# A row softmax on one core: sixteen 4 MB tiles issued by a tile framework become eleven tiles of up to 6 MB, hand-synchronised and looped

## The chip, the core and the metric

The kernel runs on one core of a Trainium2 chip. The other cores are idle. The metric is the device time of one launch in microseconds (us); lower is better. The core has a matrix engine (PE, unused here except for waits in the changed kernel), a vector engine (DVE), an activation engine (ACT), a general engine (POOL) and a sequencer for transfers (SP). Sixteen DMA engines move data between the device memory (DRAM) and the on-chip memory (SBUF, 128 partitions).

## The reference: what is computed

```python
def setup_inputs():
    batch, seq, dim = 32, 512, 1024
    return {"x": np.random.randn(batch, seq, dim).astype(np.float32), "temperature": 0.5}

def reference(x, temperature):
    scaled = x / temperature
    shifted = scaled - np.max(scaled, axis=-1, keepdims=True)
    exp_x = np.exp(shifted)
    return (exp_x / np.sum(exp_x, axis=-1, keepdims=True)).astype(np.float32)
```

There are 16,384 rows of 1,024 float32 numbers, that is 67.1 MB to read and 67.1 MB to write. A row needs its maximum, the exponential of every element, the sum, and a multiplication by the reciprocal of the sum.

## The kernel before

The rows are cut into 16 tiles of 1,024 rows (`TILES = [[8]] * 16`, L10). A tile lies in SBUF as 128 partitions by 8 rows, and the 8 rows of a partition are neighbours in DRAM, so a partition's share is one run of 32 KB. Six buffers of 4 MB each (`BUFS = 6`, L11) hold the tiles, which are worked on in place. Each tile is computed in two groups of four rows a partition (`GROUP = 4`, L13).

For a group, `maximum` (L64) lets DVE take the four row maxima in one TENSOR_REDUCE (L70) and scale them into the exponential's bias (L73). `exponential` (L75) lets ACT run four ACTIVATE instructions (L79), one a row, each of which also leaves the row's sum. `divide` (L88) lets DVE take the four reciprocals (L91) and then multiply row by row (L93). `store` (L97) lets POOL issue one transfer of the whole tile to DRAM (L101) after the tile's second group, and then calls `load` for the tile that takes the same buffer.

The order on each engine is the order in which the Python loops emit the instructions (L107 to L116): the maximum and exponential of group g, then the divide and store of group g-1. All of it is unrolled, so DVE and ACT each have a stream of more than 200 instructions. The framework adds the semaphores. Loads are issued by SP (L61): six at the start, and each later one when the store that last read its buffer has landed. Stores go out through POOL's queue, loads through SP's queue.

After the last store, SP waits for the semaphores of everything that is in flight, POOL drains its queue, and all engines meet in a barrier, clear the semaphores and meet once more. The profile gives these instructions to L147.

Of the kernel before, what the change touches and what calls it, by code (L numbers as in the profile page):

```python
# [1 line left out]

# [4 lines left out]

TILES = [[8]] * 16  # L10
BUFS = 6  # L11

GROUP = 4  # L13


@with_exitstack
def kernel(
    ctx: ExitStack,
    tc: tile.TileContext,
    x: bass.AP,  # L20
    temperature: bass.AP,
    out: bass.AP,
):
    nc = tc.nc
    f32 = mybir.dt.float32
    scale = 1.0 / float(temperature)
    extreme = mybir.AluOpType.max if scale > 0 else mybir.AluOpType.min

    P = 128
    xf = x.flatten_outer_dims()  # L30
    of = out.flatten_outer_dims()
    n, d = xf.shape
    assert sum(sum(ks) for ks in TILES) * P == n

    data = ctx.enter_context(tc.tile_pool(name="data", bufs=BUFS))
    stats = ctx.enter_context(tc.tile_pool(name="stats", bufs=4))


    groups, first, r = [], [], 0
    for i, ks in enumerate(TILES):  # L40
        first.append(r)
        r += sum(ks)
        a = 0
        for k in ks:
            for b in range(0, k, GROUP):
                m = min(GROUP, k - b)
                groups.append((i, a + b, m, (a, k) if b + m == k else None))
            a += k

    def dram(t, i):  # L50
        k = sum(TILES[i])
        block = t[P * first[i] : P * (first[i] + k), :]
        return block.rearrange("(p k) d -> p k d", p=P, k=k)

    tiles, small = [], []

    def load():
        i = len(tiles)
        if i < len(TILES):
            xt = data.tile([P, sum(TILES[i]), d], f32, name="xt")  # L60
            nc.sync.dma_start(out=xt, in_=dram(xf, i))  # L61
            tiles.append(xt)

    def maximum(g):  # L64
        i, a, k, _ = groups[g]
        top, bias, sums, recip = (
            stats.tile([P, k], f32, name=name) for name in ("top", "bias", "sums", "recip")
        )
        small.append((bias, sums, recip))
        nc.vector.tensor_reduce(  # L70
            out=top, in_=tiles[i][:, a : a + k, :], axis=mybir.AxisListType.X, op=extreme
        )
        nc.vector.tensor_scalar_mul(bias, in0=top, scalar1=-scale)  # L73

    def exponential(g):  # L75
        i, a, k, _ = groups[g]
        bias, sums, _ = small[g]
        for b in range(k):
            nc.scalar.activation(  # L79
                tiles[i][:, a + b, :],  # L80
                tiles[i][:, a + b, :],
                mybir.ActivationFunctionType.Exp,
                bias=bias[:, b : b + 1],
                scale=scale,
                accum_out=sums[:, b : b + 1],
            )

    def divide(g):  # L88
        i, a, k, _ = groups[g]
        _, sums, recip = small[g]  # L90
        nc.vector.reciprocal(recip, sums)  # L91
        for b in range(k):
            nc.vector.tensor_scalar_mul(  # L93
                tiles[i][:, a + b, :], in0=tiles[i][:, a + b, :], scalar1=recip[:, b : b + 1]
            )

    def store(g):  # L97
        i, _, _, part = groups[g]
        if part:
            a, k = part  # L100
            nc.gpsimd.dma_start(out=dram(of, i)[:, a : a + k, :], in_=tiles[i][:, a : a + k, :])  # L101
            if a + k == sum(TILES[i]):
                load()

    with tc.manual_schedule():  # L107
        for _ in range(BUFS):
            load()
        for g in range(len(groups) + 1):  # L110
            if g < len(groups):
                maximum(g)
                exponential(g)
            if g > 0:
                divide(g - 1)
                store(g - 1)  # L116


# [1 line left out]
_INS = ['x', 'temperature']  # L120
_OUTS = [((32, 512, 1024), 'float32')]

_NUMBERS = {'temperature': 0.5}


# [26 lines left out]
```

## Time and profile before

| | |
|---|---|
| median of 10 runs | 318.36 us (318.01 to 318.74) |
| profiled execution, its own time | 318.1 us |
| profiled execution, span of the program's instructions | 316.3 us |
| DVE busy | 235.5 us (74%) |
| ACT busy | 149.6 us (47%) |
| POOL busy | 8.8 us (3%) |
| moved by DMA in the span | 134.25 MB, mean 424 GB/s |
| loads and stores | 16 and 16, of 4,096 KB each |

The profile is of one execution. Its times count from the first instruction of the program, and the span ends with the program's last instruction; some 1.8 us of the execution's own time lie outside the span. An engine's busy share tells how much of the span it works, not whether it decides the end. For a kernel that mostly moves data, the busy share of the DMA engines in slices of the span, and what happens before they start and after they stop, are the first things to read. Besides the loads (queue q1) and the stores (queue q0) there is a queue of instruction packets (q14), through which the engines' programs are fetched.

### The profile page before, as it was taken

To read this page: it belongs to the slowest core of one execution; us is meant where nothing else is said; L and a number is where in the kernel's file an instruction comes from. 1 tells how busy PE (TensorE), PEld (TensorE's weight loads), DVE (VectorE), ACT (ScalarE), POOL (GpSimd) and SP (SyncE) were. 2 spreads that over 40 slices of the span, in tenths; PEclk is the share of its full clock that TensorE was granted. 3 is DMA by queue.
4 is the path that set the end of the run, shared out by engine and by line. 5 is a ranking of instruction groups with operands and counts; after the bars stand their busy time and mean duration, and the time that the engine had idled before them with its cause. 6 is when DMAs were issued, how large, how long until landed. Compare 5 with 4: busy or idle time off the path is not lost.

```text
span 316.3 us, 639 instructions
## 1 busy us (share of the span) xinstructions
DVE 235.5 (74%) x224; ACT 149.6 (47%) x257; POOL 8.8 (3%) x20
## 2 busy tenths in 40 slices
DVE  0399999999698594976949679395893958949700
ACT  0176666666546065560645516355262553625500
POOL 0000000000000000000000000000000000000000
DMA  8999999999999999999999999999999999999995
GB/s 331 410 452 423 377 460 439 423 433 431 439 423 452 410 456 406 460 402 460 410 452 431 435 427 432 452 410 456 406 460 399 464 402 460 419 443 431 431 431 240
DMA packets 4612, 134.25 MB, mean 424 GB/s; under 512 B 512, under 2 KB 512, under 8 KB 512
## 3 DMA queue, kind: packets, MB, share of 16 engines
q1 hardware_dynamic: 2304, 67.11, 49.6%
q0 software_dynamic: 2304, 67.11, 49.2%
q14 instruction: 4, 0.03, 0.0%
HBM read 67.11 MB, written 67.11 MB: 424 GB/s over the span
## 4 chain that ended last, share of the span: by engine, by line
issue 88%; DMA 4%; POOL 2%; POOLq 0%
DMA xt<-in_x_dram 4%; POOL out_dram L101 2%; POOLq L147 0%; POOLq L101 0%
## 5 line engine op out<-in xcount | busy, mean ns | idle before, releaser
L79 ACT ACTIVATE xt<-xt,bias 128x1024 f32<-128x1024 f32 x128 | 145.4, 1137 | 135.3 <-DVE recip L91 117.9
L70 DVE TENSOR_REDUCE top<-xt 128x4 f32<-128x4096 f32 x32 | 141.3, 4416 | 61.0 <-DMA xt<-in_x_dram 61.0
L93 DVE TENSOR_SCALAR xt<-xt,recip 128x1024 f32<-128x1024 f32 x128 | 87.7, 750 | 1.1
L79 ACT ACTIVATION_READ_ACCUMULATOR xt<-xt,bias 128x1 f32 x128 | 23.8, 186 | 0.0
L101 POOL DMA_DIRECT2D out_dram<-xt x16 | 8.6, 540 | 292.6 <-DVE xt L93 292.6
L79 ACT ACT_TABLE_LOAD x1 | 1.3, 1283 | 13.0 <-DMA xt<-in_x_dram 13.0
L91 DVE RECIPROCAL recip<-sums 128x4 f32<-128x4 f32 x32 | 5.5, 171 | 2.1 <-ACT xt L79 2.1
L73 DVE TENSOR_SCALAR bias<-top 128x4 f32<-128x4 f32 x32 | 5.4, 170 | 1.1
L133 POOL MEMSET const-float32-0.0<- 128x1 f32 x1 | 0.1, 99 | 0.2 <-issue 0.2
L133 POOL MEMSET const-bfloat16-1.0<- 128x1 bf16 x1 | 0.1, 102 | 0.0
L133 POOL MEMSET const-float32-1.0<- 128x1 f32 x1 | 0.1, 99 | 0.0
L133 POOL MEMSET const-uint8-127<- 128x1 uint8 x1 | 0.1, 99 | 0.0
## 6 DMA issues: line engine op xcount, KB each, us to landing
xt<-in_x_dram SPq DMA_DIRECT2D x16, 4096.0 KB, 48.5
out_dram<-xt POOLq DMA_DIRECT2D x16, 4096.0 KB, 39.5
```

The costliest lines, as they stand in the source:

```text
L70: nc.vector.tensor_reduce(out=top, in_=tiles[i][:, a : a + k, :], axis=mybir.AxisListType.X, op=extreme)
L73: nc.vector.tensor_scalar_mul(bias, in0=top, scalar1=-scale)
L79: nc.scalar.activation(tiles[i][:, a + b, :], tiles[i][:, a + b, :], mybir.ActivationFunctionType.Exp, bias=bias[:, b : b + 1], scale=scal ...
L91: nc.vector.reciprocal(recip, sums)
L93: nc.vector.tensor_scalar_mul(tiles[i][:, a + b, :], in0=tiles[i][:, a + b, :], scalar1=recip[:, b : b + 1])
L101: nc.gpsimd.dma_start(out=dram(of, i)[:, a : a + k, :], in_=tiles[i][:, a : a + k, :])
L133: nc = _bacc.Bacc("TRN2", target_bir_lowering=False, num_devices=1)
```

## The change

The tiles become ten of 12 rows a partition and a last one of 8. They live in one buffer of four slots of 12 rows ("ring"). The framework's scheduling is replaced by one hand-written section with semaphores of its own.

SP issues the loads one after another; from the fifth on, each waits for the store that last read its slot. The first load is split into two transfers: partitions 0 to 15, and partitions 16 to 127 (`AHEAD = 16`). PE executes no arithmetic; it waits for each load's semaphore in turn and then adds 1 to a counter `ready`. POOL waits for the third load before it issues the first store, and then issues the first ten stores, each when all groups of its tile are scaled. SP issues the eleventh store.

DVE runs a loop over the tiles. Inside it, one loop over the tile's groups does maxima and biases, and a second does reciprocals and multiplications, so a tile's maxima all come ahead of its divisions. ACT runs a loop over tiles and, inside, over groups. The addresses are computed in registers. Counters that a loop waits for are counted down again by the wait (`take`). A small exponential is issued on ACT ahead of its loop. At the end, the hand-written section is left without a drain of POOL, and a second section waits for the eleventh store.

```diff
-TILES = [[8]] * 16
-BUFS = 6
+TILES = [12] * 10 + [8]
+SLOTS = 4
 GROUP = 4
+AHEAD = 16
...
+    pool = ctx.enter_context(tc.tile_pool(name="data", bufs=1))
+    ring = pool.tile([P, SLOTS * most, d], f32, name="ring")
...
+    def slot(i):
+        first = most * (i % SLOTS)
+        return ring[:, first : first + TILES[i], :]
+    def take(engine, sem, count=1):
+        engine.wait_ge(sem, count).then_inc(sem, -count)
+    def loop_groups(engine, t):
+        if groups[-1] == groups[0]:
+            return engine.Fori(0, groups[0])
+        short = t // (tiles - 1) * (groups[0] - groups[-1])
+        return engine.Fori(0, groups[0] - short)
-    with tc.manual_schedule():
-        for _ in range(BUFS):
-            load()
-        for g in range(len(groups) + 1):
-            if g < len(groups):
-                maximum(g)
-                exponential(g)
-            if g > 0:
-                divide(g - 1)
-                store(g - 1)
+    with tc.tile_critical(no_gpsimd_drain=True):
+        for i in range(tiles):
+            if i >= SLOTS:
+                nc.sync.wait_ge(stored[i % SLOTS], 16 * (i // SLOTS))
+            if i == 0:
+                nc.sync.dma_start(
+                    out=slot(0)[:AHEAD], in_=dram(xf, 0)[:AHEAD]
+                ).then_inc(opened, 16)
+                nc.sync.dma_start(
+                    out=slot(0)[AHEAD:], in_=dram(xf, 0)[AHEAD:]
+                ).then_inc(loaded[0], 16)
+            else:
+                nc.sync.dma_start(out=slot(i), in_=dram(xf, i)).then_inc(loaded[i % SLOTS], 16)
+        nc.tensor.wait_ge(opened, 16)
+        for i in range(tiles):
+            nc.tensor.wait_ge(loaded[i % SLOTS], 16 * (i // SLOTS + 1)).then_inc(ready, 1)
+        nc.gpsimd.wait_ge(loaded[2], 16)
+        for i in range(tiles - 1):
+            nc.gpsimd.wait_ge(scaled, sum(groups[: i + 1]))
+            nc.gpsimd.dma_start(out=dram(of, i), in_=slot(i)).then_inc(stored[i % SLOTS], 16)
+        with nc.vector.Fori(0, tiles) as t:
+            first = t % SLOTS * most
+            take(nc.vector, ready)
+            with loop_groups(nc.vector, t) as g:
+                group = bass.ds(g * GROUP, GROUP)
+                nc.vector.tensor_reduce(
+                    out=top[:, group],
+                    in_=ring[:, bass.ds(first + g * GROUP, GROUP), :],
+                    axis=mybir.AxisListType.X,
+                    op=extreme,
+                ).then_inc(topped, 1)
+                take(nc.vector, topped)
+                nc.vector.tensor_scalar_mul(
+                    bias[:, group], in0=top[:, group], scalar1=-scale
+                ).then_inc(biased, 1)
+            with loop_groups(nc.vector, t) as g:
+                group = bass.ds(g * GROUP, GROUP)
+                take(nc.vector, summed)
+                nc.vector.reciprocal(recip[:, group], sums[:, group]).then_inc(inverted, 1)
+                take(nc.vector, inverted)
+                for b in range(GROUP):
+                    row = ring[:, bass.ds(first + g * GROUP + b, 1), :]
+                    ins = nc.vector.tensor_scalar_mul(
+                        row, in0=row, scalar1=recip[:, bass.ds(g * GROUP + b, 1)]
+                    )
+                ins.then_inc(scaled, 1)
+        nc.scalar.activation(
+            warm, nc.const_aps.tensor(0.0, (P, 1)), mybir.ActivationFunctionType.Exp
+        )
+        with nc.scalar.Fori(0, tiles) as t:
+            first = t % SLOTS * most
+            with loop_groups(nc.scalar, t) as g:
+                take(nc.scalar, biased)
+                for b in range(GROUP):
+                    row = ring[:, bass.ds(first + g * GROUP + b, 1), :]
+                    column = bass.ds(g * GROUP + b, 1)
+                    ins = nc.scalar.activation(
+                        row,
+                        row,
+                        mybir.ActivationFunctionType.Exp,
+                        bias=bias[:, column],
+                        scale=scale,
+                        accum_out=sums[:, column],
+                    )
+                ins.then_inc(summed, 1)
+        i = tiles - 1
+        nc.sync.wait_ge(scaled, sum(groups))
+        nc.sync.dma_start(out=dram(of, i), in_=slot(i)).then_inc(finished, 16)
+        for i in range(tiles - SLOTS, tiles - 1):
+            nc.sync.wait_ge(stored[i % SLOTS], 16 * (i // SLOTS + 1))
+    with tc.tile_critical(no_gpsimd_drain=True):
+        nc.sync.wait_ge(finished, 16, synchronizes=[nc.sync.lower_ap(slot(tiles - 1))])
```

More of the change, by code (lines that the diff above doesn't have):

```diff
@@ L32 @@
     n, d = xf.shape
[L33 to L48, printed above, removed]
@@ L50, in dram @@
-    def dram(t, i):
[L51 to L67, printed above, removed]
-        )
[L69 to L102, printed above, removed]
-                load()
-    with tc.manual_schedule():
-        for _ in range(BUFS):
-            load()
-        for g in range(len(groups) + 1):
-            if g < len(groups):
-                maximum(g)
-                exponential(g)
-            if g > 0:
-                divide(g - 1)
-                store(g - 1)
+    tiles, most = len(TILES), max(TILES)
@@ new lines @@
+    assert sum(TILES) * P == n and all(k % GROUP == 0 for k in TILES)
+    groups = [k // GROUP for k in TILES]
+    assert all(g == groups[0] for g in groups[:-1]) and groups[-1] <= groups[0]
+    pool = ctx.enter_context(tc.tile_pool(name="data", bufs=1))
+    ring = pool.tile([P, SLOTS * most, d], f32, name="ring")
+    top = pool.tile([P, most], f32, name="top")
+    bias = pool.tile([P, most], f32, name="bias")
+    sums = pool.tile([P, most], f32, name="sums")
+    recip = pool.tile([P, most], f32, name="recip")
@@ new lines @@
+    warm = pool.tile([P, 1], f32, name="warm")
+    loaded = [tc.alloc_semaphore(f"loaded{s}") for s in range(SLOTS)]
+    stored = [tc.alloc_semaphore(f"stored{s}") for s in range(SLOTS)]
+    opened, ready, topped, biased, summed, inverted, scaled, finished = (
+        tc.alloc_semaphore(name)
+        for name in (
+            "opened", "ready", "topped", "biased", "summed", "inverted", "scaled", "finished",
+        )
+    )
+    def dram(t, i):
+        rows = t[P * sum(TILES[:i]) : P * sum(TILES[: i + 1]), :]
+        return rows.rearrange("(p k) d -> p k d", p=P, k=TILES[i])
@@ new lines, in slot @@
+    def slot(i):
[56 more added lines that the diff above has]
+            warm, nc.const_aps.tensor(0.0, (P, 1)), mybir.ActivationFunctionType.Exp
+        )
+        with nc.scalar.Fori(0, tiles) as t:
[12 more added lines that the diff above has]
+                        accum_out=sums[:, column],
+                    )
+                ins.then_inc(summed, 1)
[4 more added lines that the diff above has]
+            nc.sync.wait_ge(stored[i % SLOTS], 16 * (i // SLOTS + 1))
```

## The prediction, made before the changed kernel ran

> **What bounds the kernel now.** I read first the page's slices and queues, because the kernel computes little for each byte. The digits are the busy tenths of the DMA engines; a queue's line gives packets, MB and its share of sixteen engines' span.
>
> ```profile
> DMA  8999999999999999999999999999999999999995
> ...
> q1 hardware_dynamic: 2304, 67.11, 49.6%
> q0 software_dynamic: 2304, 67.11, 49.2%
> q14 instruction: 4, 0.03, 0.0%
> ```
>
> Loads (q1) and stores (q0) together take 98.8% of all sixteen engines' time; only the first and the last slice are not full. Next the table of stretches (us; then busy time of DVE, ACT and POOL; the clock; the DMA share; GB/s).
>
> ```profile
> 0.00:1.00 1.00, 0.00 (x0) 0.00 (x0) 0.20 (x4) 1.00 0.00 0
> 1.00:13.00 12.00, 0.01 (x1) 0.00 (x0) 0.00 (x0) 1.00 0.97 393
> ...
> 40.00:290.00 250.00, 200.10 (x191) 126.61 (x219) 7.44 (x14) 1.00 1.00 432
> ...
> 304.00:313.00 9.00, 0.00 (x0) 0.00 (x0) 0.00 (x0) 1.00 0.95 411
> 313.00:316.30 3.30, 0.00 (x0) 0.00 (x0) 0.00 (x0) 1.00 0.03 10
> ```
>
> The middle runs at 432 GB/s with no gap, so 134.2 MB cost 310.7 us whatever the engines do. Only some 5.6 us of the span are something else: about 2 at the start and 3 at the end. Then the waits:
>
> ```profile
> DVE top L70 <- DMA xt<-in_x_dram: 61.0, 12, 13.0
> ```
>
> ```profile
> SPq L61 <- DMA out_dram<-xt: 225.2, 10, 53.6
> ```
>
> DVE waits for loads, and loads wait for a buffer's store; no engine holds the transfers up. Last, what stands at the end: the timeline's last store, and the closing line's own instructions (ns, first and last start).
>
> ```profile
> 298.09 2.74 DVE L93 TENSOR_SCALAR xt<-xt,recip 128x1024 f32<-128x1024 f32 x4
> 301.13 0.53 POOL L101 DMA_DIRECT2D out_dram<-xt  x1 [11.72 <-DVE xt L93]
> ```
>
> ```profile
> L147 SPq EVENT_SEMAPHORE  x11: 17/28/28, 314.9 to 316.3; - x11
> L147 POOLq EVENT_SEMAPHORE  x4: 17/17/17, 315.6 to 316.2; - x4
> L147 POOLq DRAIN  x3: 34/101/14465, 301.1 to 316.1; - x3
> ```
>
> The last store is issued at 301.1 and is 9.7 us of transfer at 432 GB/s, yet transfers run to past 313: it found some 2.4 us of older stores ahead of it, so no gap opened.
>
> I also followed the trace's packet records engine by engine. A packet is one partition's 32,768 B and takes 1,213 ns; a completion packet of 4 B takes 9 ns. Fourteen engines write their last byte's completion at 313.0 to 313.4, the other two at 314.16 and 314.51. Those two carried the four instruction packets of q14 (8,192 B, 309 ns each, at 65.0, 65.0, 192.5 and 240.0), two each, and the data packet after each was 0.2 to 0.4 us late. So the kernel's last 1.1 us are two of sixteen engines finishing alone. Every engine's first packet took about 1.95 us, and around the first store (35 to 37) every engine lost about another 0.7 us.
>
> [...]
>
> **Part by part.** The sum is made against the profiled execution: 318.1 us, of which 316.3 are the span; the median of the runs is 0.26 above it.
>
> *Loops in short programs.* No engine's program reaches far enough to fetch while data flows, so the two late engines end with the others: 314.5 - 313.4 = 1.1 us less, all on the path.
>
> *Larger packets.* A partition's run becomes 48 KB. An engine's packets fall from 256 to 2 x (10 x 8 + 8) = 176. If each has a fixed part, it is at most the 9 ns of a 4-byte packet: 80 x 9 = 0.7 us; at least nothing. I take 0.4 us less.
>
> *DVE and ACT.* A group costs DVE 288.49 - 281.10 = 7.39 us by the timeline. The loop adds, for a group, two waits of DVE on itself, two loop ends[...], and register arithmetic. In the trace a dependent hop between engines is 30 to 40 ns and SP's waits follow each other every 61 ns; I estimate 0.25 to 0.3 for each self-wait with its lost overlap[...], 0.85 in all, bounds 0.3 and 1.8. The cover: a tile's load and store are 12.58 MB, 29.1 us, against 3 x 8.25 = 24.8 us of DVE. It is used up when first landing + 32 groups + last store fill the transfers' span: the first tile lands at 0.74 + 2.5 (the 12.2 of the first landing before less 9.7) + 14.6 = 17.8, so (313.5 - 17.8 - 11.2) / 32 = 8.9 us a group, 1.5 above today. Below that the cost is nothing; beyond it each 0.1 us costs 3.2. ACT has 4.6 us a group and stays shorter. The exponential put ahead and PE's counting (a hop of 0.04 us) lie beside the first transfer and cost nothing; without cover the table load is 1.3 us.
>
> *The first store's extra wait.* On POOL all later stores are queued behind it, and SP's fifth load waits for its landing. The third tile lands at 17.8 + 2 x 14.6 = 47; the four slots hold loads until 60, so transfers never run dry: nothing. Its second tile is ready by about 70 and the first store lands near 76, so the store queue is fed too. Without this cover each us of delay would cost one. The 0.7 us lost around the first store I leave as they are.
>
> *Last store on SP.* It is moved out of POOL's queue, behind loads that are all issued by then. The last load (4.2 MB) lands near 270, DVE is free at 276, and two groups bring the store to 292 or 293, with some 11 us of the tenth store still to move beside it: more cover than the 2.4 us of before.
>
> *Ends.* Before, SP walked through nine more waits (9 x 61 ns = 0.55 us) after the last landing, POOL's drain ended at 315.57, and two barriers followed, 0.25 and 0.45 us. Removed: about 0.5 us. Added: the leave of one section and the entry and leave of a second, 0.25 to 0.45 each, partly while the last store still moves. Bounds 0.6 better and 1.0 worse; I take 0.2 better. At the start, entering the section may cost a barrier (0.3 us), while a first transfer of 16 packets should be issued sooner than one of 128 (372 ns of issue before; up to 0.3): bounds 0.4 either way, I take 0.1 better.
>
> Sum: 1.1 + 0.4 + 0.2 + 0.1 = 1.8 us less, 316.3 for the profiled execution and 316.5 for the median.
>
> **Rivals.** *Few ports for the first 16 partitions (slower).* The place is the first load. [...] It decides as soon as that first packet costs over 1.8 us extra. [...] Against: no run here shows that engines sharing a port stall each other at this size.
>
> *The ends eat the gain.* If the three section edges cost 0.4 each on the path, the start 0.3 more and larger packets bring nothing: 318.4 - 1.1 + 1.2 - 0.5 + 0.3 = 318.3. For it: each barrier in the trace is of that size. Against: most edges can pass while stores move.
>
> *DVE becomes the bound.* At 1.8 us added a group: 316.5 + 3 x 3.2 = 326. For it: DVE is the busiest engine, 74%. Against: most register work can run while 0.75 us multiplications do.
>
> *The loops fetch after all.* Some 80 back-edges at about 0.6 us on one engine (309 ns and the late packet): up to 48 us, 340 and more. Against: bodies are short.
>
> **How the numbers follow.** Forecast 0.55; ports 0.20; ends 0.11; DVE 0.10; fetches 0.04. The likeliest case's own range is 315.5 to 317.7 (all bounds good: 1.1 + 0.7 + 0.6 + 0.4 less). The range reaches to 323.5 to take in most of the ports' case; what it leaves out is most of DVE's and the fetches' and the edges of the others. A measurement of this kernel can tell about 0.2%, 0.64 us, from no change: faster 0.55, same 0.12, slower 0.33.
>
> **What would show it.** In the changed profile: q14 without packets after the first microseconds, all engines' last completions within 0.5 us; 48 KB packets near 1.82 us; DVE groups near 8.25 us and DVE still waiting for loads; the last store issued near 292; SP's first issue near 0.7 to 1.0. The ports' case shows as a low DMA rate in the first 10 us[...]. The forecast is wrong if the middle drops below 432 GB/s, or a gap opens between stores at the end.

## The result, and the profile after

The changed kernel takes 333.23 us (333.04 to 333.83), the kernel before 318.32 in the runs beside it: a ratio of 1.047, interval 1.0461 to 1.0479. That is slower by 14.9 us and outside the predicted range of 315.5 to 323.5. The profiled execution took 333.48 us, of which 331.7 are the span.

The page after, slices and queues:

```profile
DMA  9989999999999999999999999999999999999996
...
q1 hardware_dynamic: 1744, 71.30, 54.8%
q0 software_dynamic: 1440, 62.92, 43.8%
```

The DMA engines look as busy as before: loads and stores together have 98.6% of their time, against 98.8%, and the queue of instruction packets is gone. A busy DMA engine is not a moving one, though. The table of stretches (us; then busy time of DVE, ACT and POOL; the clock; the DMA share; GB/s) shows it:

```profile
1.00:13.00 12.00, 0.00 (x0) 1.40 (x2) 0.00 (x0) 1.00 1.01 160
13.00:33.00 20.00, 0.00 (x0) 0.00 (x0) 0.00 (x0) 1.00 0.99 253
33.00:40.00 7.00, 4.52 (x2) 0.00 (x0) 0.00 (x0) 1.00 0.93 400
40.00:290.00 250.00, 211.18 (x198) 136.74 (x236) 4.92 (x9) 1.00 1.00 432
...
318.00:330.00 12.00, 0.00 (x0) 0.00 (x0) 0.00 (x0) 1.00 0.87 354
```

From 40 us on the rate is that of before, 432 GB/s. In the first 33 us it is 160 and then 253, at a DMA share of 0.99 to 1.01. Before, the first of these stretches ran at 393 GB/s, and the second was this:

```profile
13.00:33.00 20.00, 19.65 (x17) 13.61 (x22) 0.04 (x1) 1.00 1.02 441
```

The waits of DVE and POOL follow from that. L70 is the line of the helper `take`, so "DVEq L70" stands for a wait of DVE on one of the kernel's own counters; ahead of the first row maximum of a tile (`top`, L109) that is the wait for the tile's load.

```profile
POOL out_dram L102 <- DMA ring<-in_x_dram: 63.5, 1, 63.5
DVE top L109 <- DVEq L70: 35.2, 1, 35.2
```

DVE's first row maximum starts at 35.2 us instead of 13.0. It waits once, for the first tile, and never for a load again: 61.0 us of waits for loads before, 35.2 now, all at the start. Its work then goes on without a long gap to the last store, here from the timeline:

```profile
35.23 4.42 DVE L109 TENSOR_REDUCE top<-ring  x1 [35.23 <-DVEq L70]
39.90 0.17 DVE L116 TENSOR_SCALAR bias<-top  x1 [0.24 <-DVEq L70]
...
40.82 4.42 DVE L109 TENSOR_REDUCE top<-ring  x1 [0.75 <-issue]
...
316.70 0.35 SPq L155 DMA_DIRECT2D out_dram<-ring  x1
```

That is (316.70 - 35.23) / 32 = 8.80 us a group of four rows, of which there are 32. Two stories fit so far: the transfers were 15 us behind from the start and never won them back, or DVE, started late and slowed by its loop, set the end.

### The profile page after: what moved, and what is told of

The parts are those of the page before. It is cut to its first block, busy times and chain, and to the rows that moved or that the text cites. A ratio compares the mean times of both kernels' runs of the same rounds, so it can differ in the third digit from the quotient of the medians.

```text
span 331.7 us, 1879 instructions
## 1 busy us (share of the span) xinstructions
DVE 237.5 (72%) x224; ACT 149.9 (45%) x258; POOL 5.7 (2%) x14
## 5 line engine op out<-in xcount | busy, mean ns | idle before, releaser
L142 ACT ACTIVATE ring<-ring,bias x128 | 145.4, 1136 | 162.3 <-ACTq L70 162.3
L109 DVE TENSOR_REDUCE top<-ring x32 | 141.4, 4418 | 50.5 <-DVEq L70 35.2
L126 DVE TENSOR_SCALAR ring<-ring,recip x128 | 87.7, 749 | 13.2 <-DVEq L70 13.2
L142 ACT ACTIVATION_READ_ACCUMULATOR ring<-ring,bias x128 | 23.9, 187 | 0.0
L122 DVE RECIPROCAL recip<-sums x32 | 5.5, 173 | 8.0 <-DVEq L70 8.0
L116 DVE TENSOR_SCALAR bias<-top x32 | 5.5, 171 | 7.4 <-DVEq L70 7.4
L102 POOL DMA_DIRECT2D out_dram<-ring x10 | 5.5, 545 | 292.7 <-DVE ring L126 229.2
```

Source lines behind the costliest of these rows:

```text
L102: nc.gpsimd.dma_start(out=dram(of, i), in_=slot(i)).then_inc(stored[i % SLOTS], 16)
L109: nc.vector.tensor_reduce(out=top[:, group], in_=ring[:, bass.ds(first + g * GROUP, GROUP), :], axis=mybir.AxisListType.X, op=extreme,).th ...
L116: nc.vector.tensor_scalar_mul(bias[:, group], in0=top[:, group], scalar1=-scale).then_inc(biased, 1)
L122: nc.vector.reciprocal(recip[:, group], sums[:, group]).then_inc(inverted, 1)
L126: ins = nc.vector.tensor_scalar_mul(row, in0=row, scalar1=recip[:, bass.ds(g * GROUP + b, 1)])
L142: ins = nc.scalar.activation(row, row, mybir.ActivationFunctionType.Exp, bias=bias[:, column], scale=scale, accum_out=sums[:, column],)
```

## The experiments

The ratios are to the kernel before, run on the same chip beside each. "Ports" in the expectations is the author's name for a supposition: that a transfer's rate depends on which partitions it spans. No run here shows any ports.

### The first load as one transfer

```diff
-                nc.sync.dma_start(
-                    out=slot(0)[:AHEAD], in_=dram(xf, 0)[:AHEAD]
-                ).then_inc(opened, 16)
-                nc.sync.dma_start(
-                    out=slot(0)[AHEAD:], in_=dram(xf, 0)[AHEAD:]
-                ).then_inc(loaded[0], 16)
+                nc.sync.dma_start(out=slot(0), in_=dram(xf, 0)).then_inc(loaded[0], 16)
...
-        nc.tensor.wait_ge(opened, 16)
```

> The changed kernel with its first load as one transfer over 128 partitions. Theory 1 (ports: the split of the first load costs some 15 us of all transfers, the trace shows 160 GB/s in the first 12 us and 253 in the next 20): 316.5 to 318, first tile landed near 18 us, rate 432 GB/s from the start. Theory 2 (the looped engines or the section's edges cost the time, the slow first load being hidden by four slots of buffers): 330 or more.

Measured: 319.42 us, ratio 1.0036 (1.0024 to 1.0048). Its stretches:

```profile
1.00:13.00 12.00, 0.00 (x0) 1.40 (x2) 0.00 (x0) 1.00 0.98 393
13.00:33.00 20.00, 11.97 (x5) 7.71 (x13) 0.00 (x0) 1.00 1.00 433
33.00:40.00 7.00, 5.34 (x9) 6.10 (x12) 0.00 (x0) 1.00 1.04 449
```

The same DMA share, but 393 and 433 GB/s. So the split of the first load costs 333.23 - 319.42 = 13.8 us, nearly the whole loss. By the stretches, the split kernel moved 9.8 MB by 40 us (12 x 160 + 20 x 253 + 7 x 400) and this one 16.5 MB; the 6.7 MB between them are 15.6 us at 432 GB/s. The kernel is still slower than before, and 1.4 us above the upper end of what theory 1 expected. That remainder is taken up below.

### The loops unrolled, with and without the split

```diff
-        with nc.vector.Fori(0, tiles) as t:
+        for t in range(tiles):
-            with loop_groups(nc.vector, t) as g:
+            for g in range(groups[t]):
...
-        with nc.scalar.Fori(0, tiles) as t:
-            with loop_groups(nc.scalar, t) as g:
+        for t in range(tiles):
+            for g in range(groups[t]):
```

> The changed kernel, split first load kept, with DVE's and ACT's loops unrolled, so that addresses are constants and no branch or register step is left; the waits stay. Theory 1 (ports): 332 to 334, because the transfers lost at the start cannot be won back. Theory 2 (DVE without a gap from 35 to 317 is the bound, at 8.8 us a group where 7.4 were needed before): DVE ends some 10 to 20 us sooner and the time falls to 315 to 323.

Measured with the split: 333.84 us, ratio 1.0493 (1.0477 to 1.0509). DVE has its slack back, and the time does not fall. DVE's waits ahead of the first maximum of a tile, and the issue of the last store:

```profile
DVE top L109 <- DVEq L70: 65.4, 7, 34.3
```

```profile
312.99 0.35 SPq L155 DMA_DIRECT2D out_dram<-ring  x1
```

DVE now waits for loads seven times, and the last store is issued 3.7 us sooner than in the looped kernel without any gain. The second story, DVE as the bound of the changed kernel, is refuted.

> First load whole and both loops unrolled. Against the looped kernel with the whole load it gives the price of the loops: if they only save instruction packets, this one is about 1.1 us slower, with four or more instruction packets and one or two DMA engines that end 1 us after the rest; if the loops slow DVE onto the path, this one is faster by up to 3 us.

Measured without the split: 319.73 us, ratio 1.0044 (1.0030 to 1.0058), against 1.0024 to 1.0048 for the looped kernel with the whole load. The intervals overlap. The loops' saving, forecast as 1.1 us, is 0.3 at the most likely and not told apart from nothing. Why, the packet records show. They don't name engines; an engine's packets follow one another without a break, and the figures here for single DMA engines come from joining each packet to the one that ends where it begins. Unrolled, five instruction packets of 8 KB are back while data moves, and one engine ends at 316.5, 1.6 us after the next. But in the looped kernel with the whole load, which fetches none, one engine also ends late, at 316.0, 1.4 us after the next.

### The split by rows instead of partitions

```diff
-                    out=slot(0)[:AHEAD], in_=dram(xf, 0)[:AHEAD]
+                    out=slot(0)[:, :4], in_=dram(xf, 0)[:, :4]
...
-                    out=slot(0)[AHEAD:], in_=dram(xf, 0)[AHEAD:]
+                    out=slot(0)[:, 4:], in_=dram(xf, 0)[:, 4:]
```

> The changed kernel with its first load still split in two transfers, but by rows: rows 0 to 3 of all 128 partitions, then rows 4 to 11. Theory 1 (ports): [...]nothing is lost and the time is that of the whole load within 0.5 us, 316.5 to 318. Rival (any second transfer or the early semaphore costs it): 325 or more.

Measured: 319.09 us, ratio 1.0027 (1.0017 to 1.0037), 0.33 below the whole load. Two transfers and an early semaphore cost nothing; what costs is which partitions a transfer spans.

### Partition ranges measured by themselves

```diff
+PARTS = [(0, 128), (0, 16), (16, 128), (0, 64), (32, 96), (0, 112), (0, 32), (0, 96)]
...
+        for low, high in PARTS:
+            nc.sync.dma_start(
+                out=slot(0)[low:high], in_=dram(xf, 0)[low:high]
+            ).then_inc(opened, 16)
+            n_done += 16
+            nc.sync.wait_ge(opened, n_done)
+        nc.sync.dma_start(out=dram(of, 0), in_=slot(0)).then_inc(finished, 16)
...
```

> No softmax at all: eight loads of 48 KB a partition, each waited for before the next is issued, and one store. The partitions are 0 to 127, 0 to 15, 16 to 127, 0 to 63, 32 to 95, 0 to 111, 0 to 31, 0 to 95. Theory 1 (ports[...]): 0 to 127 at about 430 GB/s, [...]0 to 63 and 0 to 31 at 215, and 32 to 95, which has as many partitions as 0 to 63[...], at about 430; 16 to 127 at about 216 as in the changed kernel. Rival (rate falls with the number of partitions or descriptors whatever the ports): 32 to 95 is as slow as 0 to 63.

This program was executed once. SP issues each load when the one before has landed, so the distance between two starts in its timeline is the time of a load (the first column is the start, and the ranges are in the order of `PARTS`):

```profile
0.96 0.39 SPq L82 DMA_DIRECT2D ring<-in_x_dram  x1
18.57 0.34 SPq L82 DMA_DIRECT2D ring<-in_x_dram  x1
28.28 0.32 SPq L82 DMA_DIRECT2D ring<-in_x_dram  x1
55.12 0.56 SPq L82 DMA_DIRECT2D ring<-in_x_dram  x1
73.22 0.55 SPq L82 DMA_DIRECT2D ring<-in_x_dram  x1
84.03 0.33 SPq L82 DMA_DIRECT2D ring<-in_x_dram  x1
108.61 0.32 SPq L82 DMA_DIRECT2D ring<-in_x_dram  x1
118.50 0.31 SPq L82 DMA_DIRECT2D ring<-in_x_dram  x1
...
142.91 0.37 SPq L87 DMA_DIRECT2D out_dram<-ring  x1
```

All 128 partitions take 17.61 us, of which 14.56 are 6.29 MB at 432 GB/s; the rest, 3.05, I take from each:

| partitions | MB | us | GB/s less 3.05 us | median packet, us |
|---|---|---|---|---|
| 0 to 127 | 6.29 | 17.61 | 432 (by definition) | 1.82 |
| 0 to 15 | 0.79 | 9.71 | 118 | 6.06 |
| 16 to 127 | 5.51 | 26.84 | 231 | 3.36 |
| 0 to 63 | 3.15 | 18.10 | 209 | 3.84 |
| 32 to 95 | 3.15 | 10.81 | 405 | 1.82 |
| 0 to 111 | 5.51 | 24.58 | 256 | 3.29 |
| 0 to 31 | 1.57 | 9.89 | 230 | 3.82 |
| 0 to 95 | 4.72 | 24.41 | 221 | 3.80 |

The 3.05 us are rough for the short loads. The last column needs no such subtraction: it is the time of one packet, one partition's 49,152 B, by the packet records.

The pair in the middle decides. Partitions 0 to 63 and 32 to 95 are the same number with the same bytes and packets, and one takes 18.1 us and the other 10.8. A packet of 0 to 63 takes 3.84 us, about twice the 1.82 of 32 to 95, and 0 to 31 has packets like those of 0 to 63 (3.82). So the number of partitions does not set the rate alone; which ones they are counts. Why they do is not shown: 16 to 127 runs at 231 GB/s, little more than half of the full rate, with 48 partitions more than 32 to 95, and the packet records name neither engines nor partitions.

### The kernel before, with this split alone

```diff
-            nc.sync.dma_start(out=xt, in_=dram(xf, i))
+            if i == 0:
+                nc.sync.dma_start(out=xt[:16], in_=dram(xf, 0)[:16])
+                nc.sync.dma_start(out=xt[16:], in_=dram(xf, 0)[16:])
+            else:
+                nc.sync.dma_start(out=xt, in_=dram(xf, i))
```

> The kernel before with nothing changed but its first load, split into partitions 0 to 15 and 16 to 127. Theory 1 (ports): the loss is that of the changed kernel's first tile scaled by its size, 15 x 8/12 = 10 us, so 327 to 330. Rival (the loss needs the looped kernel, whose DVE has no slack to catch up): 318 to 320.

Measured: 326.45 us, ratio 1.0252 (1.0237 to 1.0267), 8.1 us more than before. Its stretches:

```profile
1.00:13.00 12.00, 0.00 (x0) 0.00 (x0) 0.00 (x0) 1.00 1.03 216
13.00:33.00 20.00, 9.86 (x6) 6.76 (x10) 0.00 (x0) 1.00 0.96 341
```

The split needs no loop and no change of tile to do harm. The size was expected at 10 us and is 8.1. Per MB of the first tile that is 1.9 us (8.1 for 4.2 MB), where the changed kernel lost 2.2 (13.8 for 6.3).

### The last store, and the wait for the third load

Both have the whole first load.

```diff
-        nc.sync.wait_ge(scaled, sum(groups))
-        nc.sync.dma_start(out=dram(of, i), in_=slot(i)).then_inc(finished, 16)
+        nc.gpsimd.wait_ge(scaled, sum(groups))
+        nc.gpsimd.dma_start(out=dram(of, i), in_=slot(i)).then_inc(finished, 16)
```

> Whole first load, and the last store issued by POOL behind the tenth instead of by SP. In the kernel with the whole load 11 of 16 DMA engines lost 0.7 us at 304, when SP's store began. Theory A (beginning a store on the loads' queue costs that): 0.5 to 0.8 us less than with the whole load alone, 318.6 to 318.9. Theory B (the last store on POOL comes later and is drained later): the same or slower, 319.4 or more.

Measured: 319.06 us, ratio 1.0025 (1.0016 to 1.0035) against 1.0024 to 1.0048: a little lower, intervals overlapping. In the packet records the late packets at 304 (8.2 us in all over eleven engines) are gone, but now eight engines stand idle there for 0.2 to 0.8 us: the tenth store is done before the last one begins. One DMA engine still ends at 315.8 where the other fifteen end by 314.1, so what the loss of the others was worth is hidden by the late one.

```diff
-        nc.gpsimd.wait_ge(loaded[2], 16)
```

> Whole first load, and the first store doesn't wait for the third load. The first store is issued near 44.5 instead of 47.8. Theory A (that wait is hidden by loads, as forecast): the same, 319.2 to 319.6. Theory B (a first store amid two loads costs each engine more than the 1.2 us it costs now): 319.9 or more.

Measured: five runs from 319.43 to 322.19, median 319.96, and one of 324.41; the ratio, without that one, is 1.0053 (1.0040 to 1.0066). The median just reaches theory B's bound, and the interval overlaps that of the whole load, so the kernel is more scattered, but not shown to be slower. Theory B's reason does not hold: the packets around the first store are late by 9.4 us in all, against 18.9 with the wait. In the profiled execution, of 322.19 us, two DMA engines fall behind all through the kernel and end 1.6 and 3.3 us after most of the others, which had themselves stood idle for 2 to 3 us before the last store. Why this run, and not those with the wait, has such engines is open.

### Tile size and loops apart

```diff
-TILES = [12] * 10 + [8]
-SLOTS = 4
+TILES = [8] * 16
+SLOTS = 6
```

This on the looped kernel with the whole load and POOL's last store:

> The looped kernel with a whole first load and POOL's last store, but in 16 tiles of 8 rows and six slots, as in the kernel before. It differs from before by loops and hand-made waits alone. Theory A (the 12-row tiles cost the remaining 0.8 us, by a dearer first store): 317.0 to 317.8, because no instruction packets are left to delay two DMA engines by 1.1 us. Theory B (looped engines cost a DMA engine as much as the fetches did, by data packets of one engine that are each some 10 to 70 ns late): 318.3 to 319.5.

Measured: 328.43 us, ratio 1.0321 (1.0307 to 1.0334). Both theories miss it by 8.9 us or more. DVE's timeline in the middle, two groups being a tile:

```profile
163.51 4.41 DVE L103 TENSOR_REDUCE top<-ring  x1
168.16 0.17 DVE L110 TENSOR_SCALAR bias<-top  x1 [0.24 <-DVEq L70]
168.85 4.42 DVE L103 TENSOR_REDUCE top<-ring  x1 [0.52 <-issue]
173.50 0.17 DVE L110 TENSOR_SCALAR bias<-top  x1 [0.23 <-DVEq L70]
174.07 0.18 DVE L116 RECIPROCAL recip<-sums  x1 [0.40 <-DVEq L70]
174.66 2.74 DVE L120 TENSOR_SCALAR ring<-ring,recip  x4 [0.41 <-DVEq L70]
178.99 0.18 DVE L116 RECIPROCAL recip<-sums  x1 [1.59 <-DVEq L70]
179.58 2.74 DVE L120 TENSOR_SCALAR ring<-ring,recip  x4 [0.41 <-DVEq L70]
182.24 4.41 DVE L103 TENSOR_REDUCE top<-ring  x1
```

A tile takes 182.24 - 163.51 = 18.73 us, 9.36 a group. Added to the arithmetic are the waits for itself (0.24 and 0.41), the loop end with its register steps (0.52), and, with only two groups in a tile, 1.59 us of waiting for ACT's second group of exponentials. The transfers for a tile need 19.4 us, so the pace would just do; but DVE starts at 13.8 and has no room to catch up: 13.8 + 32 x 9.36 = 313.3, and the last store was issued at 313.68 with nothing left to move beside it. By the packet records all sixteen DMA engines stand idle for some 9 us before it. Here DVE is the bound.

```diff
-            with loop_groups(nc.vector, t) as g:
+            for g in range(groups[0]):
...
-            with loop_groups(nc.scalar, t) as g:
+            for g in range(groups[0]):
```

> As the looped kernel with 8-row tiles, but with the two groups of a tile written out inside the loop over tiles, so that DVE and ACT execute fewer branches and register steps. Theory A (tile size): the same as with inner loops within 0.3 us. Theory B (what the sequencers execute is what slows one DMA engine): 0.3 to 1.0 us less than with inner loops, and the slow engine's lag near 1 us instead of 2.

Measured: 318.37 us, ratio 1.0006 (0.9998 to 1.0014): the time of before. DVE's timeline:

```profile
153.08 4.41 DVE L103 TENSOR_REDUCE top<-ring 128x4 f32 x1
...
170.49 4.41 DVE L103 TENSOR_REDUCE top<-ring 128x4 f32 x1
```

17.41 us a tile, 8.70 a group. The 0.66 us a group that this saves, the price of the inner loops, are worth 10.1 us. Against the kernel before, loops over tiles with hand-made waits bring nothing measurable, though no instruction packet is left.

Next, tile size alone on the kernel before:

```diff
-TILES = [[8]] * 16
-BUFS = 6
+TILES = [[12]] * 10 + [[8]]
+BUFS = 4
```

> The kernel before, unrolled and scheduled by the framework as it was, with ten tiles of 12 rows and one of 8 in four buffers. It differs from before by tile size alone. Forecast's term (larger packets: 80 x 9 ns = 0.7 us less): 317.5 to 317.9. Theory A (12-row tiles cost more than they save): 318.6 or more.

Measured: 318.92 us over 22 runs, scattered from 317.96 to 321.15, ratio 1.0031 (1.0015 to 1.0046). No run reaches the 317.5 to 317.9 forecast for the larger packets, and the lowest is no lower than the lowest of before (318.01) to speak of. In the profiled execution, one of the slower ones at 320.64 us, one DMA engine's packets are late again and again, and it ends 1.1 us after the rest. The rest had themselves stood idle for some 3 us, because a tile has landed only when its slowest engine is done: fourteen engines had finished the last load by 280.4, the last one at 282.5. DVE takes the last tile's maximum ahead of the tenth tile's last division, so the tenth store was issued only at 290.6, when most engines had nothing left to store.

Last, the rows' split and POOL's last store, as diffed above, in one kernel:

> The changed kernel with its first load split by rows over all partitions, and its last store on POOL. The two changes alone gave 319.09 and 319.06 against 319.42; if both gains add up 318.6 to 318.8, else 319.0 to 319.2. The time before (318.3) is not reached by either.

Measured: 319.46 us, ratio 1.0038 (1.0025 to 1.0051), above both ranges that were named. The two small gains don't add; none of the versions tried beats the kernel before.

## Why the prediction was wrong, point by point

**What bounds the kernel** was read rightly: transfers at 432 GB/s, before and after. That is why bytes not moved in the first 33 us are paid for in full.

**The first load's split** is the step that failed. The sum counted it under *Ends* as a first transfer of 16 packets that "should be issued sooner than one of 128", up to 0.3 us better, and gave the slower movement of these transfers no term; it cost 13.8 us. Nor was it issued sooner: the issue took 383 ns, against the 372 of before. A slow first load stood in the text as a rival with 0.20 of the chance, set aside because no run showed engines stalling each other; nor did any run show its price or its ports. Its sign came: a low rate, 160 GB/s from 1 to 13 us, with packets of 5.5 to 6.5 us for the first 16 partitions, where one takes 1.82 at the full rate. By themselves 0 to 15 move at about 118 GB/s. Why they do is not shown.

The rival's price was too low as well. By themselves the 16 partitions cost (9.71 - 3.05) - 1.82 = 4.8 us over a full-rate transfer, and the 112 others (26.84 - 3.05) - 12.74 = 11.0; the first tile landed at 34.6. Together that is 15.9, against 15.6 from the stretches, where the range allowed for 7.0 (323.5 - 316.5). That the time lost is 13.8 fits with what only the kernel with the whole load loses: 1.2 us at its first store, and most of the late engine's 1.4.

**DVE.** The added cost of a group was estimated at 0.85 us and measures 8.80 - 7.39 = 1.41, inside its bounds, so the group takes 8.80 and not 8.25. Of its parts, DVE's wait on itself is 0.24 us after a maximum and 0.41 ahead of the multiplications, where 0.25 to 0.3 was put. Loop ends and registers, which the 0.85 counts as well, were the author's estimate, with no run behind their share; in the changed kernel's trace it is 84 to 219 ns from the start of a loop's branch to DVE's next instruction. "DVE still waiting for loads" is not so: it waits for the first tile only. The limit worked out, 8.9 us a group, was only just kept: with the whole load DVE takes (302.70 - 19.1) / 32 = 8.86, one wait of 2.0 us for a load included. With 8-row tiles, which land sooner, the same working gives (313.5 - 13.8 - 11.2) / 32 = 9.0; the loop takes 9.36 and costs 10 us, so the rival of DVE as the bound was real, in another tile size.

**Loops in short programs** did what they say: no instruction packet is left while data moves, against four before. The 1.1 us is not gained, since a DMA engine still ends late in the looped kernels (316.0 against 314.6 with the whole load, 314.8 against 313.7 with loops over 8-row tiles). Some 70 of its packets are each mostly 10 to 70 ns longer. In the records of before, thirteen engines end by 313.4 and a fourteenth at 313.6, so the latest one was 0.9 us behind it, not 1.1.

**Larger packets** have the fixed part that was assumed: 16,384, 32,768 and 49,152 B take 611, 1,213 and 1,815 ns, a step of 602 for 16 KB and 9 left over. By that, 80 packets fewer are 0.7 us. No run shows them as a gain; tile size alone made the kernel slower.

**The first store's wait** costs nothing that shows, as forecast; without it the kernel is more scattered, which was not forecast. "The 0.7 us lost around the first store I leave" was wrong for the whole load: 18.9 us over sixteen engines, 1.2 each. In the changed kernel itself no late packets stand there.

**Last store on SP.** It was to come at 292 or 293 with 11 us of the tenth store beside it. It came at 316.7, and at 302.7 with the whole load, where four DMA engines stand idle for 0.1 to 0.3 us before it: the cover was all but gone. Its start made packets late by some 8 to 9 us over eleven or twelve engines.

**Ends.** SP's last instructions after the landing take no less than before (1.8 us to the end of the span). The first issue is at 0.95 instead of 0.74.

So with the split removed, 319.4 stands where the text had 316.5. Late by the records: 0.5 at the first store, 0.7 at SP's last store, 0.2 at the start, and the late engine in place of the 1.1 gained. This is a sum read from one trace; leaving out SP's last store or the loops brought no share back that shows. Which of the looped kernel, its larger packets or the recording of more executed instructions (1,879 in the changed kernel against 639) makes one engine late was not settled. Neither of the first two is needed for it: the kernel before with 48 KB packets has a late engine without a loop, and the loops over 8-row tiles have one with 32 KB packets.

## What to carry to other kernels

Split a transfer along the rows, not along the partitions: here the split by rows took 319.09 us and the one by partitions 333.23. By themselves, loads that leave out part of the 128 partitions ran at 118 to 256 GB/s where all 128 run at 432 (only 32 to 95 came near, at 405), and in this kernel, bound by transfers, nothing later made it good. When a rival has a price and no run speaks for the forecast's own term, the rival's price belongs in the sum. A loop's price is per trip: work out at what time of a trip the engine's end meets that of the transfers, and leave more room than here. The looped groups took 8.8 us against a limit of 8.9 without harm, and 9.4 against 9.0 at a cost of 10 us.

## What the runs showed that was not expected

A DMA share of 1.0 went with 160 GB/s: busy time of DMA engines does not tell that data moves at full rate, and GB/s has to be read beside it. A load of 112 partitions in one transfer ran at 231 GB/s and one of 96 at 221; one of 64, from partition 32 on, ran at 405. The kernel before with 48 KB packets scattered by 1%, with one DMA engine behind; with its 32 KB packets by 0.2%.
